# Strassen products for the gate and up projections, without GpSimd in the feed-forward; meta keys padded to 128 rows

## The chip, the cores and the metric

The kernel runs on one core of a Trainium2 chip. The metric is device microseconds of one execution; lower is better. The core's engines are TensorE (PE: matmuls; PEld: its weight loads), VectorE (DVE), ScalarE (ACT), GpSimd (POOL) and SyncE (SP, which issues the DMAs).

## The reference

A sequence of 512 tokens with 1024 features goes through a first block (two attention branches over the tokens and 16 "meta" tokens in front of them, 8 heads each) and then through two hybrid layers. Each hybrid layer has four mixing branches, an output projection and a gated feed-forward:

```python
x = x + merged.astype(dt) @ w_out
h2 = rms_norm(x, norm2_g)
ffn = (jax.nn.silu(h2 @ w_ffn_gate) * (h2 @ w_ffn_up)) @ w_ffn_down     # 1024 -> 2816 -> 1024
return x + ffn
```

## The kernel before

Activations lie transposed in SBUF: partitions are 128 features of a k-tile, the free axis is tokens. Every fp32 operand is split into a high part (a cast to fp32r) and a low part (the rest), and every product is three matmuls: high by high, high by low, low by high (`mm3`). Weights arrive by DMA into `raw` tiles (512 KB, three buffers); `split_w` casts 512 columns to `whi` on ACT and subtracts to get `wlo` on POOL (three buffers of each; with `k.lo` set, part or all of the subtractions go to DVE). `evict_split` does the same to a PSUM bank on ACT and DVE.

PE's order is the order of the program's text (a manual schedule). The order on the other engines is set at build time by a scheduler; each engine then runs its own queue in order, and waits on semaphores.

The feed-forward (`ffn`, line numbers from 1055 on) works on 22 blocks of 128 hidden features (`KF`). A block is a gate projection and an up projection, each 8 k-tiles by three matmuls of 512 tokens into one PSUM bank (`proj_t`, L248 to L250), then `silu2` (L353 ACT tanh, L354 DVE), a DVE multiply (L1067), a cast to `yh` (L1069 ACT) and a subtraction to `yl` (L1070 POOL). After every two blocks, `down` multiplies them by the down weights: two halves of 512 output features, four token tiles, three matmuls each (`proj_n`, L296 to L298), and `add_resid` (L497) adds each of the four banks to `x` on DVE. The whole of a `down` stands in PE's order between two projections. The last four blocks go through `proj_resid`, which also computes the sums of squares for the next norm; its weights are split by L557 (ACT) and L558 (POOL).

In front of the feed-forward, `proj_resid` for `w_out_2` ends each token tile with `norm_tile`: a norm (L527 DVE), eight transposes (L314 PE) and two `evict_split`s into `act`. The last tile's second half of this work runs inside the first gate block (`proj_late`, L278), which does tokens 0 to 255, the transposes, and then tokens 256 to 511 in 24 matmuls of 256 columns each.

In the first block, `Head.pv` (L443) multiplies probabilities by values for each of 16 heads, twice a head: keys in 128-row blocks, and first the 16 meta keys (`vm`, `pm`), with 16 rows on both operands.

Of the kernel before, what the change touches and what calls it, by code (L numbers as in the profile page):

```python
# [11 lines left out]
F32 = mybir.dt.float32  # L12
F32R = mybir.dt.float32r
AF = mybir.ActivationFunctionType
ALU = mybir.AluOpType
# [3 lines left out]
P = 128  # L19
S = 512  # L20
D = 1024
KD = D // P
# [45 lines left out]
class Task:  # L68
    def __init__(self, gen, cost):
        self.gen, self.left, self.done = gen, cost, False  # L70
# [89 lines left out]
def pe_cost(n):  # L160
    return max(n / 2.4 + 3, 110)
# [3 lines left out]
def hybrid_kernel(ctx: ExitStack, tc: tile.TileContext, i: dict, out: bass.AP):  # L165
# [59 lines left out]
    def raw_tile():  # L225
        return new(pool, [P, 1024], "raw", bufs=3)
# [8 lines left out]
    def w_cols(ap):  # L235

        loads, _, per, nk, _ = ap.shape
        for a in range(loads):
            raw = raw_tile().rearrange("p (m k c) -> p m k c", m=per, k=nk)
            nc.sync.dma_start(raw, ap[a])  # L240
            for m in range(per):
                yield raw[:, m]

    def mm3(ps, sh, sl, mh, ml, first, last):

        T_.matmul(ps, sh, mh, start=first, stop=False)  # L248
        T_.matmul(ps, sh, ml, start=False, stop=False)  # L249
        T_.matmul(ps, sl, mh, start=False, stop=last)  # L250

    def proj_t(outs, raw, nk):

# [142 lines left out]
    class Head:  # L396
# [7 lines left out]
        def trans(self, t, p, col):  # L404

            if t % 2 == 0:
                self.pt[t // 2] = [new(pool, [P, 4, 256], n, F32R) for n in ("pth", "ptl")]
                if self.meta:
                    k.pm_turn = 256 - k.pm_turn
                    self.pm[t // 2] = [a[0:NMETA, k.pm_turn:k.pm_turn + 256] for a in k.pm]  # L410
# [12 lines left out]
            if self.meta and t % 2:  # L423
                evict_split(self.pmt, *self.pm[t // 2])

        def pv(self, t):

# [95 lines left out]
    def norm_tile(x, t, ss, dst, gain):  # L523
# [12 lines left out]
        return second  # L536

    def proj_resid(get, ap, k0, nk, on_tile, delay=1):

        pss = [[bank(), bank()] for _ in range(NT)]  # L540
        for kk in range(nk - 4):
# [5 lines left out]
        ws = []  # L547
        for kk in range(nk - 4, nk):
            raw = load_w(ap, k0 + kk, 1, 0, D)[:, 0]
            if kk % 2:  # L550
# [84 lines left out]
def first_body(k, fb, col, hl):  # L635
# [63 lines left out]
        fox.rows = k.rows_out(fl, "frows")  # L699

    def v_tiles():
        v, vm = new(pool, [P, NT, 8, 2, 64], "v", F32R, 1), new(fb, [NMETA, 8, 2, 64], "vm", F32R)

        def put(t, ps, h0=0):
            src = ps.rearrange("p (h d) -> p h d", d=64)
            dst = (v[:, t] if t < NT else vm)[:, h0:h0 + src.shape[1]]
# [51 lines left out]
    def fox_values():  # L758
# [262 lines left out]
def hybrid_layer(k, spill, h, l, last):  # L1021
# [19 lines left out]
    def on_tile(t, pss):  # L1041
        for half, ps in enumerate(pss):
            k.add_resid(x, t, half, ps, ss)
        return k.norm_tile(x[:, t], t, ss, act, gain)

    k.proj_resid(lambda kk, t: tuple(a[:, kk, t * P:(t + 1) * P] for a in act), i["w_out_2"][l], 0, KD, on_tile)
    return ffn(k, x, l, act, last)


def ffn(k, x, l, h, last):  # L1050
    nc, i, new, V, A_, f, pool, bank, stream = k.nc, k.i, k.new, k.V, k.A_, k.f, k.pool, k.bank, k.stream
    gw, uw = (k.w_cols(i[n][l]) for n in ("t_gate", "t_up"))
    wd = i["w_ffn_down_2"][l]

    def get(kk):
        return h[0][:, kk], h[1][:, kk]

    def block(last=False):
        pg = bank()
        for _ in k.proj_t([(pg, get)], next(gw), KD):  # L1060
            pass
        gt = k.silu2(pg, k.t2())
        pu = bank()
        for _ in k.proj_t([(pu, get)], next(uw), KD):
            pass
        pr = k.t2()
        V.scalar_tensor_tensor(pr, pu, 0.5, gt, ALU.mult, ALU.mult)  # L1067
        hi, lo = k.y_tile()
        A_.copy(hi, pr)  # L1069
        (V if last else k.G).tensor_tensor(lo, pr, f(hi), ALU.subtract)  # L1070
        return hi, lo

    def down(a, acts):
        for half in range(2):
            pss = k.four()
            outs = [(pss[t], lambda kk, t=t: tuple(b[:, t * P:(t + 1) * P] for b in acts[kk])) for t in range(NT)]
            for _ in k.proj_n(outs, wd, len(acts), half * 512, 512, k0=a):
                pass
            for t in range(NT):
                k.add_resid(x, t, half, pss[t])  # L1080


    pending = None
    for a, n in [(a, 2) for a in range(0, KF - 4, 2)] + [(KF - 4, 4)]:
        acts = []
        for j in range(n):
            acts.append(block(j == 3))
            if pending:
                down(*pending)
                pending = None  # L1090
        pending = (a, acts)

    ss = new(k.small, [P, 8], "xss")
    gain = k.gain_row(i["final_g_2"] if last else i["norm1"][l + 1], "cb")
# [15 lines left out]
    k.proj_resid(lambda kk, t: tuple(b[:, t * P:(t + 1) * P] for b in acts[kk]), wd, KF - 4, 4, on_tile)  # L1110
    return (None, None) if last else (spill, h)


# [743 lines left out]
```

## Time and profile before

| | |
|---|---|
| time, median of three runs | 2608.05 us (2605.62 to 2610.39) |
| the profiled execution's own time, and its span | 2611.06 us; 2608.8 us |
[...]
| busy: PE, PEld, DVE, ACT, POOL | 2538.1, 2117.7, 1335.3, 1163.9, 1291.9 us |
| feed-forward of the first hybrid layer | about 1111 to 1486 us of the span |
| feed-forward of the second | about 2235 to 2609 us |

The span is from the first to the last instruction of the profiled execution; its time is a little longer, as it holds the launch around it. [...]

### The profile page before, as it was taken

Reading aid. Unit: us, or ns where it says so; the run is one execution under the profiler, and the core shown is the slowest. Engines: PE = TensorE matmul, PEld = TensorE weight load, DVE = VectorE, ACT = ScalarE, POOL = GpSimd, SP = SyncE. Lnnn points to the kernel's source line nnn. Section 1 sums busy time; section 2 is a strip of 40 time slices with the busy share of each in tenths; the row PEclk is TensorE's granted clock in tenths of the full one; section 3 lists DMA queues with packets and bytes.
Section 4 is the critical chain, followed back from the end, with each engine's and each line's share of the span. In section 5 each row is a group of like instructions: output and inputs, shape, how many; then the busy total and the mean of one; then the engine's idle time right before and its main releaser. Section 6 shows DMA issues by size and latency. Waiting matters only on the chain. (4 is left out here: it accounts for less than half of the span.)

```text
span 2608.8 us, 36327 instructions
## 1 busy us (share of the span) xinstructions
PE 2538.1 (97%) x12918; PEld 2117.7 (81%) x12918; DVE 1335.3 (51%) x2895; ACT 1163.9 (45%) x2533; POOL 1291.9 (50%) x1112
## 2 busy tenths in 40 slices
PE   7999999999999999999999999999999999999998
PEld 7878788888888878788888887888888877888887
DVE  4577547869436465522222469685355574322223
ACT  4567645447435444332222455365354453322223
POOL 3443245552466544455555555424665535455554
PEclk9999999999999999999999999999999999999999
DMA  5542242222437332322222332224364324222322
GB/s 152 147 127 65 75 134 95 80 88 64 137 105 188 112 109 82 137 89 97 97 96 93 110 108 76 88 64 121 118 187 119 99 88 143 82 92 96 97 97 89
DMA packets 117733, 276.98 MB, mean 106 GB/s; under 512 B 15824, under 2 KB 37584, under 8 KB 117552
## 3 DMA queue, kind: packets, MB, share of 16 engines
q1 hardware_dynamic: 117552, 274.65, 34.5%
q8 instruction: 103, 1.69, 0.3%
q14 instruction: 78, 0.64, 0.1%
HBM read 230.26 MB, written 6.46 MB: 91 GB/s over the span
## 5 line engine op out<-in xcount | busy, mean ns | idle before, releaser
L222 POOL TENSOR_TENSOR wlo<-raw,whi 128x512 fp32r<-128x512 f32 (+2 forms) x721 | 925.2, 1285 | 886.1 <-ACT whi L220 870.0
L220 ACT CAST whi<-raw 128x512 fp32r<-128x512 f32 (+2 forms) x733 | 445.0, 609 | 815.6 <-PE A L249 475.3
L248 PE MATMUL A<-hi,whi 128*128 128x512 f32 (+1 forms) x1848 | 741.0, 401 | 0.7 <-ACT hi L210 0.7
L250 PE MATMUL A<-hi,wlo 128*128 128x512 f32 (+1 forms) x1848 | 722.5, 391 | 6.0 <-POOL wlo L222 6.0
L249 PE MATMUL A<-lo,whi 128*128 128x512 f32 (+1 forms) x1848 | 724.4, 392 | 0.1
L250 PEld LDWEIGHTS A<-hi,wlo 128*128 128x128 f32 x1848 | 348.2, 188 | 85.6 <-POOL wlo L222 8.6
L248 PEld LDWEIGHTS A<-hi,whi 128*128 128x128 f32 x1848 | 348.5, 189 | 64.9 <-ACT hi L210 0.8
L249 PEld LDWEIGHTS A<-lo,whi 128*128 128x128 f32 x1848 | 348.6, 189 | 63.4 <-DVE lo L211 0.3
L314 PE MATMUL A<-ident,p 128*128 128x128 f32 (+3 forms) x1125 | 176.2, 279 | 31.3 <-DVE p L527 16.3
L497 DVE TENSOR_TENSOR x<-x,A 128x512 f32<-128x512 f32 x176 | 119.9, 688 | 157.7 <-PE A L298 96.4
L211 DVE TENSOR_TENSOR ptl<-A,pth 128x512 fp32r<-128x512 f32 (+3 forms) x256 | 149.1, 583 | 89.9 <-ACT pth L210 88.7
L314 PEld LDWEIGHTS A<-ident,p 128*128 128x128 f32 (+3 forms) x1125 | 135.2, 139 | 71.5 <-DVE p L527 17.7
L354 DVE SCALAR_TENSOR_TENSOR t<-t,A 128x512 f32<-128x512 f32 x44 | 30.3, 688 | 251.8 <-ACT t L353 251.8
L332 ACT ACTIVATE p<-p,sm 128x512 f32<-128x512 f32 (+6 forms) x160 | 100.6, 629 | 128.9 <-DVE sm L331 128.3
L210 ACT CAST pth<-A 128x512 fp32r<-128x512 f32 (+3 forms) x256 | 128.2, 501 | 64.9 <-PE A L314 64.2
L296 PE MATMUL A<-whi,hi 128*128 128x256 f32 (+7 forms) x440 | 144.2, 328 | 0.0
L310 POOL TENSOR_TENSOR rstd<-rstd,mhalf 128x1 f32<-128x1 f32 (+2 forms) x80 | 56.7, 710 | 175.5 <-DVE rstd L309 168.3
L298 PE MATMUL A<-whi,lo 128*128 128x256 f32 (+7 forms) x440 | 141.4, 321 | 0.0
L297 PE MATMUL A<-wlo,hi 128*128 128x256 f32 (+7 forms) x440 | 141.3, 321 | 0.0
L1067 DVE SCALAR_TENSOR_TENSOR t<-A,t 128x512 f32<-128x512 f32 x44 | 30.4, 692 | 172.5 <-PE A L250 172.5
L296 PE MATMUL A<-whi,yh 128*128 128x512 f32 x288 | 112.2, 390 | 0.0
L297 PE MATMUL A<-wlo,yh 128*128 128x512 f32 x288 | 112.2, 390 | 0.0
(365 smaller groups left out, 4565.5 us busy)
## 6 DMA issues: line engine op xcount, KB each, us to landing
raw<-in_t_gl_dram SPq DMA_DIRECT2D x64, 512.0 KB, 3.5
raw<-in_t_gate_dram SPq DMA_DIRECT2D x44, 512.0 KB, 3.4
raw<-in_t_up_dram SPq DMA_DIRECT2D x44, 512.0 KB, 3.5
raw<-in_w_ffn_down_dram SPq DMA_DIRECT2D x44, 512.0 KB, 3.7
raw<-in_w_in_dram SPq DMA_DIRECT2D x26, 512.0 KB, 3.7
raw<-in_w_out_dram SPq DMA_DIRECT2D x24, 512.0 KB, 3.6
ks<-sth SPq DMA_DIRECT2D x64, 128.0 KB, 2.4
ks<-stl SPq DMA_DIRECT2D x64, 128.0 KB, 2.3
```

The costliest lines, as they stand in the source:

```text
L210: A_.copy(hi, ps)
L211: V.tensor_tensor(lo, ps, f(hi), ALU.subtract)
L220: A_.copy(hi, src)
L222: (V if k.lo and k.turn % k.lo == 0 else G).tensor_tensor(lo, src, f(hi), ALU.subtract)
L248: T_.matmul(ps, sh, mh, start=first, stop=False)
L249: T_.matmul(ps, sh, ml, start=False, stop=False)
L250: T_.matmul(ps, sl, mh, start=False, stop=last)
L296: T_.matmul(ps, sh, wh[:, j], start=(b + j == 0), stop=False)
L297: T_.matmul(ps, sh, wl[:, j], start=False, stop=False)
L298: T_.matmul(ps, sl, wh[:, j], start=False, stop=(b + j == nk - 1))
L314: T_.transpose(dst, src, ident[0:k, 0:k])
L497: V.tensor_tensor(xx, xx, ps, ALU.add)
```

## The change

**Meta keys.** `vm` and `pm` get 128 partitions instead of 16, zeroed once by POOL memsets, so the meta matmuls contract over 128 rows.

**Quarters.** `norm_tile` in front of the feed-forward copies each transposed tile a second time, unsplit, to four fp32 "quarters" (k-tiles 0 to 3 or 4 to 7, tokens 0 to 255 or 256 to 511): eight ACT copies of 128x512 a layer.

**Gate and up by pairs of blocks.** Two blocks of a projection are a 2 by 2 product of quarters. `fast_pair` computes it in seven products instead of eight (Strassen's scheme in Winograd's form), each of 4 k-tiles by three matmuls of 256 tokens. `Tokens.sums` forms the four sums of token quarters once a layer and splits them; `fast_pair` forms four sums of weight quarters a pair (`s1` to `s4`) and splits the seven weight operands. Three PSUM banks (`px`, `pw`, `pz`) take the products, with ACT copies and DVE adds in between. The first pair's gate stays plain. So a layer has 21 fast pairs.

**Engines.** In the feed-forward every two-operand step stands on DVE (`k.lo` is 1; 2 during the plain pair), none on POOL until the last `proj_resid`.

**Down by fours.** `down` takes four blocks at a time and is a generator in the stream: after each product (12 matmuls) about one group of three 512-column matmuls is taken from it. It runs during the two pairs after its blocks are made; nothing runs between the products of the first two pairs.

```diff
     def v_tiles():
-        v, vm = new(pool, [P, NT, 8, 2, 64], "v", F32R, 1), new(fb, [NMETA, 8, 2, 64], "vm", F32R)
+        v, vm = new(pool, [P, NT, 8, 2, 64], "v", F32R, 1), new(fb, [P, 8, 2, 64], "vm", F32R)
+        G.memset(f(vm), 0.0)
...
     k.pm, k.pm_turn = k.y_tile(), 0
+    for a in k.pm:
+        G.memset(f(a), 0.0)
...
-                evict_split(ps.rearrange("p (j c) -> p j c", j=4), *(d[:, 4 * half:4 * half + 4, t * P:(t + 1) * P] for d in dst))
+                src = ps.rearrange("p (j c) -> p j c", j=4)
+                evict_split(src, *(d[:, 4 * half:4 * half + 4, t * P:(t + 1) * P] for d in dst))
+                if quarters:
+                    A_.copy(quarters[half][t // 2][:, :, (t % 2) * P:(t % 2 + 1) * P], src)
...
+        def sums(self):
+            (b11, b12), (b21, b22) = self.q
+            hi = new(pool, [P, 4, 4, 256], "v", F32R, 1)
+            lo = [new(pool, [P, 2, 4, 256], "ks", F32R) for _ in range(2)]
+            self.t = [(hi[:, j], lo[j // 2][:, j % 2]) for j in range(4)]
+            for c in (slice(0, 2), slice(2, 4)):
+                t = [t2().rearrange("p (k c) -> p k c", k=2) for _ in range(4)]
+                V.tensor_tensor(t[0], b12[:, c], b11[:, c], ALU.subtract)
+                V.tensor_tensor(t[1], b22[:, c], t[0], ALU.subtract)
+                V.tensor_tensor(t[2], b22[:, c], b12[:, c], ALU.subtract)
+                V.tensor_tensor(t[3], b21[:, c], t[1], ALU.subtract)
+                for j in (1, 2, 0, 3):
+                    A_.copy(self.t[j][0][:, c], t[j])
+                    V.tensor_tensor(self.t[j][1][:, c], t[j], f(self.t[j][0][:, c]), ALU.subtract)
...
+    def fast_pair(raw1, raw2, tok, dst):
+        a11, a21, a22, a12 = raw1[:, 0:4], raw2[:, 0:4], raw2[:, 4:8], raw1[:, 4:8]
...
+        A_.copy(h1, raw1)
+        V.tensor_tensor(l1, raw1, f(h1), ALU.subtract)
+        V.tensor_tensor(s1, a21, a22, ALU.add)
+        V.tensor_tensor(s2, s1, a11, ALU.subtract)
+        V.tensor_tensor(s3, a11, a21, ALU.subtract)
+        V.tensor_tensor(s4, a12, s2, ALU.subtract)
...
+        yield product(px, (h1[:, 0:4], l1[:, 0:4]), tok.quarter(0, 0))
+        A_.copy(q, px)
+        yield product(pw, (h1[:, 4:8], l1[:, 4:8]), tok.quarter(1, 0))
+        V.tensor_tensor(d1[:, 0:256], q, pw, ALU.add)
+        yield product(px, split(s2), t2_, False)
+        A_.copy(u2, px)
+        yield product(pz, split(s1), t1)
+        A_.copy(z, pz)
+        yield product(px, split(s3), t3, False)
+        V.tensor_tensor(d2[:, 256:512], z, px, ALU.add)
+        yield product(pz, split(s4), tok.quarter(1, 1), False)
+        V.tensor_tensor(d1[:, 256:512], u2, pz, ALU.add)
+        yield product(px, split(a22), t4, False)
+        A_.copy(d2[:, 0:256], px)
...
+    def fast(w):
+        dst = [k.t2() for _ in range(2)]
+        for cost in k.fast_pair(next(w), next(w), tok, dst):
+            stream.run(cost * rate)
+        return dst
...
+        if first:
+            k.lo = 2
+            gts = [k.silu2(plain(gw), k.t2()) for _ in range(2)]
+            tok.sums()
+            k.lo = 1
+        else:
+            gts = [k.silu2(g, g) for g in fast(gw)]
...
+    rate = 2 * NT * 2 * 3 * k.pe_cost(S) / (14 * 12 * k.pe_cost(256))
```

Two places show what moves on DVE. The first is the start of the feed-forward in the first hybrid layer. Before, DVE's queue from the first gate block on holds (`t` is the silu's and the product's tile, `A` a PSUM bank, `x` the residual):

```order
L354 SCALAR_TENSOR_TENSOR t_2664_12233<-t_2665_12234,A_12160 128x512
L1067 SCALAR_TENSOR_TENSOR t_2672_12272<-A_12237,t_2664_12233 128x512
L354 SCALAR_TENSOR_TENSOR t_2681_12313<-t_2682_12314,A_12278 128x512
L1067 SCALAR_TENSOR_TENSOR t_2689_12352<-A_12317,t_2681_12313 128x512
L354 SCALAR_TENSOR_TENSOR t_2698_12393<-t_2699_12394,A_12358 128x512
L1067 SCALAR_TENSOR_TENSOR t_2706_12432<-A_12397,t_2698_12393 128x512
```

Now, behind the second gate block's silu, the queue goes on with the token sums (L560 to L563, `t`; first their columns c = 0 to 1, then 2 to 3) and their low parts (L566, `ks`); ahead of these rows stand the silu and three sums `t_2681`, `t_2682`, `t_2683`. The third product of the first fast pair needs the low parts of the second sum, made from `t_2682` and `t_2686`:

```order
L566 TENSOR_TENSOR ks_12293<-t_2681_12295,v_12292 128x512
L563 TENSOR_TENSOR t_2684_12298<-cst_11794,t_2682_12296 128x512
L587 TENSOR_TENSOR ptl_12622<-raw_12613,pth_12621 128x1024
L560 TENSOR_TENSOR t_2685_12311<-qs_11793,qs_11792 128x512
L566 TENSOR_TENSOR ks_12293<-t_2682_12296,v_12292 128x512
L566 TENSOR_TENSOR ks_12294<-t_2683_12297,v_12292 128x512
L566 TENSOR_TENSOR ks_12294<-t_2684_12298,v_12292 128x512
L561 TENSOR_TENSOR t_2686_12312<-cst_11795,t_2685_12311 128x512
L566 TENSOR_TENSOR ks_12293<-t_2685_12311,v_12292 128x512
L562 TENSOR_TENSOR t_2687_12313<-cst_11795,qs_11793 128x512
L563 TENSOR_TENSOR t_2688_12314<-cst_11794,t_2686_12312 128x512
L588 TENSOR_TENSOR p_12477<-qs_12475 128x512
```

The next row is `ks_12293<-t_2686_12312`. What moved: where the queue held one or two instructions a block, each behind a matmul, it now holds a run of 16 between the second gate's silu and that row.

The second place is the middle of the feed-forward. Before, DVE's queue there is two multiplies a block and the adds to `x`:

```order
L354 SCALAR_TENSOR_TENSOR t_2750_12637<-t_2751_12638,A_12602 128x512
L1067 SCALAR_TENSOR_TENSOR t_2758_12676<-A_12641,t_2750_12637 128x512
L497 TENSOR_TENSOR x_11778<-x_11778,A_12682 128x512
L497 TENSOR_TENSOR x_11778<-x_11778,A_12683 128x512
L497 TENSOR_TENSOR x_11778<-x_11778,A_12684 128x512
```

Now (`wlo` from L581 is the low part of a product's weights, from L222 that of the down weights; L588 to L591 are the sums for the next pair; L606 and L612 add a product's bank):

```order
L606 TENSOR_TENSOR t_2880_13293<-t_2893_13314,A_13312 128x256
L222 TENSOR_TENSOR wlo_13394<-raw_13328,whi_13393 128x512
L581 TENSOR_TENSOR wlo_13402<-p_13301,whi_13401 128x512
L590 TENSOR_TENSOR p_13483<-raw_13477,qs_13479 128x512
L581 TENSOR_TENSOR wlo_13422<-p_13302,whi_13421 128x512
L498 TENSOR_TENSOR x_11782<-x_11782,A_13150 128x512
L591 TENSOR_TENSOR p_13484<-raw_13477,p_13482 128x512
L612 TENSOR_TENSOR t_2881_13294<-t_2894_13315,A_13311 128x256
L581 TENSOR_TENSOR wlo_13442<-qs_13297,whi_13441 128x512
```

What moved: the subtractions that POOL did, and all new sums, stand in one DVE queue, 40 instructions for a gate pair and an up pair together, and each `wlo` is awaited by the product after it.

## Rows read from the trace of the kernel before

**Rows 1.** Windows of both feed-forwards: stretch, us, busy us (instructions), PEclk, DMA, GB/s
```profile
1118.00:1456.00 338.00, 338.00 (x1472) 275.86 (x1471) 78.77 (x115) 103.50 (x172) 190.93 (x149) 1.00 0.30 99
2241.00:2580.00 339.00, 339.00 (x1479) 276.75 (x1478) 79.08 (x116) 103.51 (x172) 191.37 (x150) 1.00 0.30 97
```

**Rows 2.** Groups of 1118 to 1456: busy us, mean ns | idle before, releaser
```profile
L222 POOL TENSOR_TENSOR wlo<-raw,whi 128x512 fp32r<-128x512 f32 x121 | 156.4, 1293 | 150.2 <-ACT whi L220 150.2
...
L220 ACT CAST whi<-raw 128x512 fp32r<-128x512 f32 x121 | 75.2, 621 | 223.5 <-PE A L249 149.2 <-PE A L298 68.7 <-PE A L250 2.4
...
L497 DVE TENSOR_TENSOR x<-x,A 128x512 f32<-128x512 f32 x72 | 49.1, 688 | 48.0 <-PE A L298 48.0
...
L558 POOL TENSOR_TENSOR ptl<-raw,pth 128x512 fp32r<-128x512 f32 x4 | 5.1, 1302 | 1.4 <-ACT pth L557 1.4
```

**Rows 3.** PE alone, a stretch of down, then of gate and up
```profile
1150.00:1157.25 7.25, 7.25 (x33) 1.00 0.21 72
1157.25:1179.52 22.27, 22.27 (x98) 1.00 0.28 95
```

**Rows 4.** Timeline of PE, second pass of the first gate block
```profile
1115.63 0.39 PE L278 MATMUL A<-hi,whi 128*128 128x256 f32 x1
1115.86 0.28 PE L278 MATMUL A<-hi,wlo 128*128 128x256 f32 x1
...
1117.62 1.11 PE L278 MATMUL A<-lo,whi 128*128 128x256 f32 x8
1118.56 0.40 PE L248 MATMUL A<-hi,whi 128*128 128x512 f32 x1
```

**Rows 5.** Timeline of PE around one meta multiplication in the first block
```profile
85.11 0.39 PE L250 MATMUL A<-hi,wlo 128*128 128x512 f32 x1
85.43 0.38 PE L443 MATMUL A<-yh,vm 16*128 16x256 f32 x1
85.65 0.27 PE L443 MATMUL A<-yl,vm 16*64 16x256 f32 x1
85.85 0.39 PE L443 MATMUL A<-pth,v 128*128 128x256 f32 x1
86.08 0.34 PE L443 MATMUL A<-ptl,v 128*64 128x256 f32 x2
```

**Rows 6.** Timeline of DVE, two independent instructions in a row
```profile
690.10 1.28 DVE L211 TENSOR_TENSOR v<-A,v 128x512 fp32r<-128x512 f32 x2
```

**Rows 7.** Instructions of line 222: count, ns min/median/max, first and last start
```profile
L222 DVE TENSOR_TENSOR wlo<-raw,whi x12: 680/690/1469, 551.7 to 1704.7; 128x512 fp32r<-128x512 f32 x12
```

**Rows 8.** Groups on DVE over the whole span, by shape
```profile
L211 DVE TENSOR_TENSOR ptl<-A,pth 128x256 fp32r<-128x256 f32 x48 | 19.9, 414 | 30.2 <-ACT pth L210 30.2
...
L1152 DVE TENSOR_TENSOR x<-x,t 128x512 f32<-128x512 f32 x16 | 25.4, 1587 | 0.2
```

**Rows 9.** Timeline of ACT and DVE at the end of the first gate block
```profile
1118.35 0.62 ACT L220 CAST whi<-raw 128x512 fp32r<-128x512 f32 x1 [2.04 <-PE A L278]
...
1118.87 0.59 ACT L353 ACTIVATE t<-A 128x512 f32<-128x512 f32 x1
...
1119.50 0.69 DVE L354 SCALAR_TENSOR_TENSOR t<-t,A 128x512 f32<-128x512 f32 x1 [2.46 <-ACT t L353]
```

**Rows 10.** Busy time and granted clock after two long waits of PE
```profile
358.00:365.00 7.00, 5.75 (x28) 5.74 (x29) 5.51 (x13) 2.49 (x6) 1.38 (x3) 0.52 0.31 120
...
412.70:416.10 3.40, 3.35 (x8) 2.67 (x9) 1.56 (x7) 2.13 (x6) 2.48 (x2) 0.52 0.46 154
```

**Rows 11.** Timeline of PE at those two waits
```profile
359.25 1.11 PE L314 MATMUL A<-ident,p 128*128 128x128 f32 x4 [4.07 <-DVE p L527]
...
412.75 0.80 PE L250 MATMUL A<-hi,wlo 128*128 128x512 f32 x1 [2.16 <-POOL wlo L222]
```

**Rows 12.** Groups on POOL over the whole span
```profile
L1282 POOL MEMSET p<- 36x512 f32 x2 | 1.0, 518 | 0.0
```

**Rows 13.** Timeline of PE at the start of the span
```profile
7.28 1.12 PE L314 MATMUL A<-ident,p 128*128 128x128 f32 x4 [7.28 <-DVE p L527]
```

More of the change, by code (lines that the diff above doesn't have):

```diff
@@ L233, in load_w, with w_cols @@
         return raw
-    def w_cols(ap):
+    def w_cols(ap, other=None):
         loads, _, per, nk, _ = ap.shape
         for a in range(loads):
-            raw = raw_tile().rearrange("p (m k c) -> p m k c", m=per, k=nk)
+            raw = (other() if other and a > 2 and a % 2 else raw_tile()).rearrange("p (m k c) -> p m k c", m=per, k=nk)
             nc.sync.dma_start(raw, ap[a])
@@ L242, in w_cols, with mm3 @@
                 yield raw[:, m]
[L246 to L250, printed above, removed]
+    def mm3(ps, sh, sl, mh, ml, first, last, **kw):
+        T_.matmul(ps, sh, mh, start=first, stop=False, **kw)
+        T_.matmul(ps, sh, ml, start=False, stop=False, **kw)
+        T_.matmul(ps, sl, mh, start=False, stop=last, **kw)
     def proj_t(outs, raw, nk):
@@ new lines, in fast_pair, with part, split, product @@
+    def fast_pair(raw1, raw2, tok, dst):
+        a11, a21, a22, a12 = raw1[:, 0:4], raw2[:, 0:4], raw2[:, 4:8], raw1[:, 4:8]
+        def part():
+            return p_tile().rearrange("p (k c) -> p k c", k=4)
+        def split(src):
+            hi, lo = (new(pool, [P, 512], t, F32R, 3).rearrange("p (k c) -> p k c", k=4) for t in ("whi", "wlo"))
+            A_.copy(hi, src)
+            V.tensor_tensor(lo, src, f(hi), ALU.subtract)
+            return hi, lo
+        s1, s2, s3, s4 = (part() for _ in range(4))
+        h1, l1 = (new(pool, [P, 4, 256], n, F32R).rearrange("p a b -> p (a b)").rearrange("p (k c) -> p k c", k=KD) for n in ("pth", "ptl"))
+        A_.copy(h1, raw1)
[4 more added lines that the diff above has]
+        V.tensor_tensor(s4, a12, s2, ALU.subtract)
+        t1, t2_, t3, t4 = tok.t
+        px, pw, pz = (bank()[:, 0:256] for _ in range(3))
+        def product(ps, w, m, first=True):
+            for j in range(4):
+                mm3(ps, w[0][:, j], w[1][:, j], m[0][:, j], m[1][:, j], first and j == 0, j == 3, skip_group_check=not first)
+            return 12 * pe_cost(256)
+        (u, v), (d1, d2) = (t2(), t2()), dst
+        q, u2, z = u[:, 0:256], u[:, 256:512], v[:, 0:256]
+        yield product(px, (h1[:, 0:4], l1[:, 0:4]), tok.quarter(0, 0))
[12 more added lines that the diff above has]
+        A_.copy(d2[:, 0:256], px)
@@ L1050, in ffn, with plain, y_tiles, pair @@
-def ffn(k, x, l, h, last):
+    return ffn(k, x, l, act, quarters, last)
+def ffn(k, x, l, h, quarters, last):
     nc, i, new, V, A_, f, pool, bank, stream = k.nc, k.i, k.new, k.V, k.A_, k.f, k.pool, k.bank, k.stream
-    gw, uw = (k.w_cols(i[n][l]) for n in ("t_gate", "t_up"))
+    gw, uw = (k.w_cols(i[n][l], lambda: new(pool, [P, 2 * L], "qs")[:, 0:1024]) for n in ("t_gate", "t_up"))
+    tok = k.Tokens(h, quarters)
     wd = i["w_ffn_down_2"][l]
+    count = [0]
     def get(kk):
         return h[0][:, kk], h[1][:, kk]
-    def block(last=False):
-        pg = bank()
-        for _ in k.proj_t([(pg, get)], next(gw), KD):
-            pass
[L1062 to L1071, printed above, removed]
+    def plain(w):
+        ps = bank()
+        for _ in k.proj_t([(ps, get)], next(w), KD):
+            pass
+        return ps
+    def fast(w):
[3 more added lines that the diff above has]
+        return dst
+    def y_tiles():
+        count[0] += 1
+        if count[0] % 8 == 0:
+            return [new(pool, [P, L], n, F32R, 1)[:, 0:S] for n in ("sth", "stl")]
+        if count[0] % 8 == 4:
+            return [k.gate_tile().bitcast(F32R) for _ in range(2)]
+        return k.y_tile()
+    def pair(first):
+        if first:
[5 more added lines that the diff above has]
+            gts = [k.silu2(g, g) for g in fast(gw)]
+        out = []
+        for u, gt in zip(fast(uw), gts):
+            V.scalar_tensor_tensor(gt, u, 0.5, gt, ALU.mult, ALU.mult)
+            hi, lo = y_tiles()
+            A_.copy(hi, gt)
+            V.tensor_tensor(lo, gt, f(hi), ALU.subtract)
+            out.append((hi, lo))
+        return out
@@ L1076, in down @@
             outs = [(pss[t], lambda kk, t=t: tuple(b[:, t * P:(t + 1) * P] for b in acts[kk])) for t in range(NT)]
-            for _ in k.proj_n(outs, wd, len(acts), half * 512, 512, k0=a):
-                pass
+            yield from k.proj_n(outs, wd, len(acts), half * 512, 512, k0=a)
             for t in range(NT):
                 k.add_resid(x, t, half, pss[t])
[L1083 to L1091, printed above, removed]
+    rate = 2 * NT * 2 * 3 * k.pe_cost(S) / (14 * 12 * k.pe_cost(256))
+    acts = []
+    for a in range(0, KF, 2):
+        acts += pair(a == 0)
+        if len(acts) >= 4 and a < KF - 4:
+            stream.drain()
+            stream.push(down(a + 2 - len(acts), acts), 0)
+            acts = []
+        elif a == KF - 4:
+            stream.drain()
+            stream.push(down(KF - 6, acts[0:2]), 0)
+            acts = acts[2:]
+    stream.drain()
+    k.lo = 0
     ss = new(k.small, [P, 8], "xss")
@@ L1108, in on_tile, with home @@
             nc.sync.dma_start(k.out[t * P:(t + 1) * P, sl], x[:, t, sl])
-    k.proj_resid(lambda kk, t: tuple(b[:, t * P:(t + 1) * P] for b in acts[kk]), wd, KF - 4, 4, on_tile)
+    homes = iter(((pool, "qs"), (k.mix, "cst")))
+    def home():
+        where, tag = next(homes)
+        return tuple(new(where, [P, 1024], tag, F32R, 2) for _ in range(2))
+    k.proj_resid(lambda kk, t: tuple(b[:, t * P:(t + 1) * P] for b in acts[kk]), wd, KF - 4, 4, on_tile, home=home)
     return (None, None) if last else (spill, h)
```

24 lines of the change are left out of this document (16 added, 8 removed).

## The prediction, made before the change had run

> **What bounds the kernel now.** I began with the windows by stage, because the share of busy time over a whole span hides its stages. In both feed-forwards PE is busy for all of the stretch, 338.00 of 338.00 us and 339.00 of 339.00, at the full granted clock, while DVE has 79 us of work, ACT 104 and POOL 191, and the DMA engines are busy for 0.30 [rows 1]. The groups say who waits for whom: POOL's subtractions (L222) stood idle 150.2 us for the casts (L220), and most idle time of these was a wait for PE's banks [rows 2]. So PE is the bound, and what counts is how long it needs from one matmul's start to the next. PE alone gives that: 96 gate and up matmuls of 512 columns in 22.27 us, 0.232 us a step, and 32 of down in 7.25, 0.227 [rows 3]. The two extra records of the first and the one extra of the second are neighbours cut by the window.
>
> **1. The products: -51 us.** Two plain blocks are 48 matmuls of 512 columns, 48 x 0.232 = 11.13 us. A fast pair is 7 x 12 = 84 matmuls of 256 columns. The trace has such matmuls in this very role: the second pass of the first gate block runs 8 of them, with new weights each, from 1117.62 to the next start at 1118.56, (1118.56 - 1117.62) / 8 = 0.118 us; the whole pass of 24 takes 1118.56 - 1115.63 = 2.93 us, 0.122 [rows 4]. At 0.118 the pair is 9.91 us, 1.22 less; 42 pairs (21 a layer) give -51. At 0.122 they would give -37, at half of 0.232, the lowest I can think of, -58. The weight loads grow from 48 to 84 a pair, and PEld has one for each matmul already [rows 1].
>
> [...] The steps of 0.118 in rows 4, each with weights of its own on all 128 rows, leave no room for a load in line, so I give it no chance.
>
> **2. The meta keys: -10 us.** In `pv` the step into the first meta matmul is 85.43 - 85.11 = 0.32 where a full matmul of 512 has 0.232, and the steps around it are 0.22, 0.20 and 0.23 where 256 columns of 128 rows take 0.118 [rows 5]. That is (0.32 - 0.232) + (0.22 + 0.20 + 0.23 - 3 x 0.118) = 0.39 us a call; with 32 calls (16 heads, twice) 12.4 us. Some calls will stand where PE waits for something else, so I take 10; bounds 0 and 12.4. [...] The zeroing is 4 memsets, about 2 us of POOL by the nearest row (518 ns for 36x512, [rows 12]), in the first microseconds, while PE's first work waits 7.28 us for a norm anyway [rows 13].
>
> **3. The start of a feed-forward: +13 us a layer, +26.** This is where a new wait arises. The second gate block's silu ends about 1.6 to 2.3 us after PE leaves that block: 1119.50 + 0.69 - 1118.56 = 1.63 at the first block [rows 9], and 0.6 more if a cast of 0.62 stands ahead. Behind it DVE has 16 rows until the low part of the second token sum: 15 of 512 columns and one of 1024. For one I have 0.69 [rows 2, 7] and, back to back, 1.28 - 0.68 = 0.60 [rows 6]; for 1024 columns at most twice that. [...] By rows the 16 take 15 x 0.60 + 1.2 = 10.2 to 15 x 0.69 + 1.38 = 11.7 us, so the sum stands at 11.8 to 14.0. PE meanwhile has two products and half of the third, 30 matmuls, 3.5 us. It waits 8.3 to 10.5 us; I take 9.7. To this come 0.7 at the seventh product, whose bank is read by L612 behind more DVE rows; 1.0 in the second pair, which has no down beside it, so DVE has 24 x 0.66 + 6 x 0.42 + 2 x 1.2 = 20.8 us of work (0.42: [rows 8]) against 168 x 0.118 = 19.8 of PE; and 1.3 for the clock: after a wait of 4.07 us PE ran at 0.52 for about 7 us, and after one of 2.16 us for 3.4 [rows 10, 11]. That is 12.7, say 13; bounds 9 and 18. Behind the waiting matmul stand all later products, and the silu, casts and down that need them, so nothing makes it up.
>
> **4. The steady state: +4 us.** From the third pair on, a gate and an up pair with their down take PE 168 x 0.118 + 48 x 0.227 = 30.7 us. DVE has 40 instructions for it: 32 of 512 columns, 6 of 256 and 2 of 1024, by the same rows 26 us at 0.66 (27 at 0.69); ACT has 28, at 0.62 about 17. POOL's 1293 ns subtractions [rows 2] are gone. So DVE would be 85% busy, in one queue, with PE waiting for each `wlo`. `whi` and `wlo` have three buffers, and the tight places are those where a buffer comes free with one product and is needed for the low part of one soon after: 12 x 0.118 of a product, 3 x 0.227 of down and two matmuls ahead of the reader, 2.3 us from release to need. Against that stand a release of 0.31 (1118.87 - 1118.56, [rows 9]), a cast of 0.62, a subtraction of 0.69, 0.04 between them as between tanh and silu there, and 0.2 that I add for the hand-over to PE: 1.9 us, with DVE free at that moment. Where DVE is in the middle of another 0.69, it is late by 0.3. I take 0.1 a fast pair for the 36 with a down: +3.6; bounds 0 and 22 (0.3 at two places of a pair).
>
> **5. The end: +2 us.** The last `proj_resid` splits its weights with POOL subtractions of 1302 ns (L558, [rows 2]) as before, but beside DVE work on two SBUF operands, which can take 1587 ns where POOL is busy (L1152, [rows 8]). I take 1 us a layer, 0 to 3. The eight quarter copies a layer are ACT work of 0.6 us at a place where ACT is busy 0.31 of the time [rows 1]; if the transposes' banks came free later by one of them, 0.6 a layer, inside these bounds. Weights come by the same DMA count, and the engines were at 0.30.
>
> **The sum.** -51.2 - 10 + 26 + 3.6 + 2 = -29.6. The profiled execution took 2611.06 us, so 2581.5 on its scale; the median of the runs is 3.0 below it, 2578.5. Forecast 2579.
>
> **The rivals.**
> A, the start's wait is hidden, since DVE gets through its 16 rows while the second gate block still runs. For it: the early sums need only tokens that are ready. Against: the silu stands ahead of them in the queue, and waits for PE. It saves about 23: 2556. Chance 0.08.
> B, the forecast. Own range 2566 to 2594. Chance 0.55.
> C, the other side: DVE becomes the bound of the steady state. Its work there is 26 / 0.66 = 39.4 times a 512-column instruction, so it passes PE's 30.7 us at a mean of 0.78 us, and eats the whole gain (29.6 over 20 gate-and-up rounds, 1.5 us each) at 0.82. For it: L1152 shows 1.59 us for two SBUF operands beside POOL, and L222's longest is 1.47 [rows 7, 8]. Against: POOL is almost idle there now, and the median is 0.69. At 0.85 a round is 33.5, +2.8 over 20 rounds: 2635. Chance 0.12.
> D, the change doesn't do what it says: half-wide matmuls don't come at half price in short runs, because each product's first step, into another bank, costs a full 0.23. For it: the first steps of the pass, 0.23 and on average 0.122 [rows 4]. Against: the 8 behind. 0.11 x 7 x 42 = +32: 2611. Chance 0.13.
> E, the tight places of the steady state bind at each pair, +0.3 at two of them, +22 instead of +3.6: 2597 to 2604. Chance 0.12.
>
> **How the numbers follow.** Some 0.2% (2602.8 to 2613.3) is what a measurement of this kernel can tell from no change. A, B and E are faster: 0.75. D is nearly all in the band: 0.10 of its 0.13 same, the rest slower, with C: 0.15. The terms' bounds taken together reach from 2555 to 2635; without C and the upper side of D, 2552 to 2612 keeps 0.8.
>
> **What would show it.** In the profile after: the steps inside products near 0.118 and PE's feed-forward busy time down by a tenth (1); steps of 0.118 in `pv` with no 0.2 (2); in each feed-forward one or two waits of PE, 9 to 10 us together, in the first products of the first fast pair, released by DVE's L566 (or L587), with a half clock behind (3); DVE 80 to 90% busy in the middle, its 512-column instructions at 0.60 to 0.69, and PE's waits there under 0.2 us each (4). The prediction is wrong if those DVE instructions exceed 0.78, if PE's waits in the middle come at every pair, or if the first step of each product is 0.2.

## The result, and the profile after

The changed kernel takes 2580.7 us, median of four runs (2576.7 to 2581.96); the kernel before took 2609.2 (2605.6 to 2611.6). The ratio is 0.9891, 95% interval 0.9877 to 0.9906. The forecast was 2579, with the sign right; the terms behind it came out less well than their sum.

To see where the time went, both traces were cut at five matmuls that exist in both: the first 512-column matmul behind each `proj_late` (in the first hybrid layer, its feed-forward's second gate block, and the same in the second layer) and the last matmul.

| stretch, us | before | after | change |
|---|---|---|---|
| start (with all meta keys) to the first layer's first projection | 369.75 | 358.21 | -11.54 |
| to the second gate block of the first feed-forward | 748.81 | 754.04 | +5.23 |
| this feed-forward, to the second layer's first projection | 370.98 | 357.24 | -13.74 |
| to the second gate block of the second feed-forward | 752.60 | 754.55 | +1.95 |
| to the last matmul | 359.29 | 347.37 | -11.92 |

So the first block gave 11.5 us and the feed-forwards 25.7, and 7.2 went in the two mixing stretches, which the change touches only at their ends (quarter copies, and the first pair's weight sums). The windows of both feed-forwards, from the second fast pair to near the end, answer to [rows 1] (columns as there):

```profile
1150.00:1430.00 280.00, 280.00 (x1973) 262.14 (x1973) 223.39 (x362) 138.89 (x260) 5.56 (x4) 1.00 0.31 101
2260.00:2540.00 280.00, 279.30 (x1969) 261.44 (x1968) 223.69 (x362) 138.90 (x261) 4.23 (x4) 1.00 0.32 103
```

PE is still the bound, with no idle time in the first and 0.7 us in the second. DVE went from 23% of such a stretch to 80%, ACT from 31% to 50%, POOL from 56% to 2%. The groups of DVE between 1150 and 1430 us (busy us, mean ns | idle before, releaser) answer to [rows 2, 7]:

```profile
L581 DVE TENSOR_TENSOR wlo<-p,whi 128x512 fp32r<-128x512 f32 x73 | 50.2, 687 | 3.3 <-ACT whi L580 1.1
L222 DVE TENSOR_TENSOR wlo<-raw,whi 128x512 fp32r<-128x512 f32 x36 | 25.2, 699 | 33.2 <-ACT whi L220 33.0
L498 DVE TENSOR_TENSOR x<-x,A 128x512 f32<-128x512 f32 x37 | 25.2, 680 | 0.0
L587 DVE TENSOR_TENSOR ptl<-raw,pth 128x1024 fp32r<-128x1024 f32 x17 | 20.8, 1223 | 5.4 <-ACT pth L586 5.2
```

The mean of a 512-column row is 0.69 us, far from the 0.78 at which DVE would have become the bound, and the 1024-column row takes 1.22, not twice 0.69.

The start of the first feed-forward is where PE waits. Its timeline from the end of the second product on:

```profile
1120.53 0.28 PE L251 MATMUL A<-hi,ptl 128*128 128x256 f32 x1
1128.12 0.58 PE L249 MATMUL A<-v,whi 128*128 128x256 f32 x1 [7.31 <-ACT t L604]
1128.49 0.41 PE L250 MATMUL A<-ks,whi 128*128 128x256 f32 x1
...
1129.56 0.41 PE L249 MATMUL A<-v,whi 128*128 128x256 f32 x1
1130.12 0.58 PE L250 MATMUL A<-ks,whi 128*128 128x256 f32 x1
...
1133.06 0.34 PE L251 MATMUL A<-v,wlo 128*128 128x256 f32 x1
1133.24 0.28 PE L249 MATMUL A<-v,whi 128*128 128x256 f32 x1
...
1136.42 0.28 PE L249 MATMUL A<-v,whi 128*128 128x256 f32 x1
...
1137.84 0.28 PE L249 MATMUL A<-hi,pth 128*128 128x256 f32 x1
```

Three things stand in these rows. PE is idle for 7.3 us in front of the third product, and ACT's copy L604 releases it. Its eighth matmul, the first that reads the low part of the second sum's later half (`ks`), comes 0.56 us after the seventh instead of 0.21: the wait that the prediction had put there, now a remainder of 0.35. And from 1128.12 to 1133.06 the steps are 0.213 (0.37 and 0.38 behind the two stops) where the later ones are 0.118: behind the wait the granted clock is 0.50 in 1128.1 to 1133.0, and 0.99 in 1133.1 to 1136.4. The third and fourth products should have started at 1120.65 and taken 24 x 0.118 = 2.83 us; the fifth starts at 1133.60, so the start costs 1133.60 - 1120.65 - 2.83 = 10.1 us: 7.5 of wait, 0.35, and about 2.3 of half clock. The seventh product (1136.42 to 1137.84, 12 steps of 0.118) and the pair behind it run without a wait.

DVE and ACT at the same place:

```profile
1119.10 0.68 DVE L355 SCALAR_TENSOR_TENSOR t<-t,A 128x512 f32<-128x512 f32 x1
1119.69 0.68 DVE L560 TENSOR_TENSOR t<-qs,qs 128x512 f32<-128x512 f32 x1
...
1124.57 1.89 DVE L566 TENSOR_TENSOR ks<-t,v 128x512 fp32r<-128x512 f32 x3
1126.37 0.68 DVE L561 TENSOR_TENSOR t<-cst,t 128x512 f32<-128x512 f32 x1
1126.97 0.68 DVE L566 TENSOR_TENSOR ks<-t,v 128x512 fp32r<-128x512 f32 x1
...
1128.78 0.68 DVE L588 TENSOR_TENSOR p<-qs 128x512 f32<-128x512 f32 x1
1129.38 1.28 DVE L566 TENSOR_TENSOR ks<-t,v 128x512 fp32r<-128x512 f32 x2
```

```profile
1127.09 0.62 ACT L565 CAST v<-t 128x512 fp32r<-128x512 f32 x1 [1.79 <-DVE t L561]
1127.69 0.37 ACT L604 COPY t<-A 128x256 f32<-128x256 f32 x1
```

DVE runs its rows back to back, a row every 0.60 us. Counted along the queue shown with the change, the low part of the second sum's later half (from `t_2686`) is the row right behind L588, the first of the two at 1129.38. It ends at 1130.06, and the eighth matmul of the third product, which reads it, starts at 1130.12. The copy that frees the bank `px` for the third product needs only the first product, done at 1119.4, but stands on ACT behind the cast L565 of the same half of that sum (L561), which DVE gets to at 1126.37.

So the copy decides where PE stops, at the product's first matmul, and DVE's 16 rows decide when the eighth can go. At 0.118 a step the eighth, 31 matmuls behind 1117.81, would have started at 1121.47; it is 8.65 us late. The other 1.5 of the 10.1 us are half clock behind it. By this count a copy in time would have brought seven matmuls forward and left the eighth where it is.

The meta multiplication of [rows 5], after:

```profile
84.75 0.39 PE L251 MATMUL A<-hi,wlo 128*128 128x512 f32 x1
84.99 0.28 PE L444 MATMUL A<-yh,vm 128*128 128x256 f32 x1
85.10 0.28 PE L444 MATMUL A<-yl,vm 128*64 128x256 f32 x1
85.22 0.28 PE L444 MATMUL A<-pth,v 128*128 128x256 f32 x1
85.33 0.33 PE L444 MATMUL A<-ptl,v 128*64 128x256 f32 x2
```

The steps are 0.24, 0.11, 0.12 and 0.11, where they were 0.32, 0.22, 0.20 and 0.23.

### The profile page after: what moved, and what is told of

It is laid out like the page before. It is cut to its first block, busy times and chain, and to the rows that moved or that the text cites. A ratio compares the mean times of both kernels' runs of the same rounds, so it can differ in the third digit from the quotient of the medians.

```text
span 2578.9 us, 39966 instructions
## 1 busy us (share of the span) xinstructions
PE 2489.7 (97%) x14430; PEld 2158.1 (84%) x14430; DVE 1718.3 (67%) x3527; ACT 1294.7 (50%) x2817; POOL 934.0 (36%) x830
## 4 chain that ended last, share of the span: by engine, by line
PE 63%; DVE 11%; DMA 3%; issue 2%; ACT 2%; POOL 2%; SPq 0%; DVEq 0%; POOLq 0%; ACTq 0%
PE A L249 14%; PE A L250 14%; PE A L251 14%; PE A L297 4%; PE A L299 4%; PE A L298 4%; PE A L315 3%; PE A L444 2%; DMA raw<-in_w_out_dram 1%; DVE x L1277 1%; PE A L489 1%; DVE ptl L211 1%; POOL wlo L222 1%; DVE sm L332 1%; POOL ptl L640 1%
## 5 line engine op out<-in xcount | busy, mean ns | idle before, releaser
L222 POOL TENSOR_TENSOR wlo<-raw,whi 128x512 fp32r<-128x512 f32 (+4 forms) x477 | 612.8, 1288 | 583.0 <-ACT whi L220 567.3
L220 ACT CAST whi<-raw 128x512 fp32r<-128x512 f32 (+4 forms) x565 | 340.8, 605 | 507.7 <-PE A L250 320.1
L249 PE MATMUL A<-hi,whi 128*128 128x512 f32 (+2 forms) x1344 | 524.6, 390 | 0.7 <-ACT hi L210 0.7
L251 PE MATMUL A<-hi,wlo 128*128 128x512 f32 (+2 forms) x1344 | 505.6, 376 | 3.1 <-POOL wlo L222 2.9
L250 PE MATMUL A<-lo,whi 128*128 128x512 f32 (+2 forms) x1344 | 505.9, 376 | 0.1
L251 PEld LDWEIGHTS A<-hi,wlo 128*128 128x128 f32 x1344 | 253.6, 189 | 54.6 <-POOL wlo L222 6.1
L249 PE MATMUL A<-v,whi 128*128 128x256 f32 x672 | 191.9, 286 | 15.3 <-ACT t L604 14.6
L251 PE MATMUL A<-v,wlo 128*128 128x256 f32 x672 | 191.1, 284 | 0.2 <-DVE wlo L581 0.2
L250 PE MATMUL A<-ks,whi 128*128 128x256 f32 x672 | 191.0, 284 | 0.3
L222 DVE TENSOR_TENSOR wlo<-raw,whi 128x512 fp32r<-128x512 f32 x88 | 64.5, 733 | 125.8 <-ACT whi L220 125.6
L249 PEld LDWEIGHTS A<-v,whi 128*128 128x128 f32 x672 | 129.1, 192 | 21.9 <-ACT t L604 15.0
```

The source lines that it names most:

```text
L220: A_.copy(hi, src)
L222: (V if k.lo and k.turn % k.lo == 0 else G).tensor_tensor(lo, src, f(hi), ALU.subtract)
L249: T_.matmul(ps, sh, mh, start=first, stop=False, **kw)
L250: T_.matmul(ps, sh, ml, start=False, stop=False, **kw)
L251: T_.matmul(ps, sl, mh, start=False, stop=last, **kw)
```

## The experiments

The theory under test: the padding gives about 10 us and the products 51; the start of each feed-forward gives 20 of that back, through DVE's queue; the steady state costs next to nothing. The rivals: other parts of the change make the gain; or the start's cost is DVE's whole work and not the order of its rows; or DVE is at its limit all along. Ratios are against the kernel before, with 95% intervals.

### The padding alone, and the change without it

```diff
+        v, vm = ..., new(fb, [P, 8, 2, 64], "vm", F32R); G.memset(f(vm), 0.0)   # e1: into the kernel before
-        v, vm = ..., new(fb, [P, 8, 2, 64], "vm", F32R); G.memset(f(vm), 0.0)   # e2: out of the changed one
```

(Shortened; the same is done with `pm`.)

> The kernel before with only the meta keys padded to 128 rows. Theory: the shorter first block of the changed kernel (about 11 us between the same two matmuls of the two traces) is the padding's alone, so about 2598 us (2595 to 2601), with steps of 0.118 us around the meta matmuls. Rival: the first block got shorter through other timing, and the padding only moves PE's time into waits for other engines; then the time stays within 4 us of 2609.

> The changed kernel with the meta keys at 16 rows again. Theory: the padding's 11 us come back and nothing else, 2592 us (2589 to 2595), and the feed-forwards keep their length within 1 us. Rival: the padding is worth less beside the rest, below 2586.

The padding alone: 2598.9 us, ratio 0.9962 (0.9948 to 0.9977), 10.3 us less than before. The change without it: 2590.4, ratio 0.9923 (0.9907 to 0.994), 9.7 more than with it. The two parts of the change add up, and the padding is worth 10 us. Both times lie in the theories' ranges.

### All blocks plain, the rest of the change kept

```diff
     def fast(w):
-        dst = [k.t2() for _ in range(2)]
-        for cost in k.fast_pair(next(w), next(w), tok, dst):
-            stream.run(cost * rate)
-        return dst
+        for _ in range(2):
+            ps = bank()
+            for cost in k.proj_t([(ps, get)], next(w), KD):
+                stream.run(cost * 0.5)
+            yield ps
...
-            tok.sums()
```

> The changed kernel with all gate and up blocks as plain products and without the token sums; the quarter copies, the engines' division and the down by fours between the products stay. Theory: the products alone give 42 x 1.22 = 51 us, and the start costs about 10 us a layer, so without both the time is 2581 + 51 - 20 = 2612 us (2607 to 2616), and no wait of PE over 1 us is left in the feed-forward. Rival: part of the gain comes from the division of engines and the down by fours, then at most 2603 us.

2632.9 us, ratio 1.0091 (1.0074 to 1.0108): 21 more than the theory's figure, and on the other side from the rival. The row of PE's waits in the first feed-forward says why (us, times, longest):

```profile
PE A L298 <- DVE wlo L222: 8.9, 18, 1.1
```

Beside plain blocks the split of the down weights comes 0.61 us late at nearly every half of a down, and the step behind it is 0.1 longer: all steps over 0.32 us of this feed-forward together, less 0.23 each, come to 14.4 us. That fault is this experiment's own: the changed kernel has no such wait. Without it the first feed-forward is 386.6 - 14.4 = 372.2 us against 371.0 before (1.8 of it in such steps), so by this subtraction the division of engines and the down by fours gain nothing by themselves. And against 357.24 - 10.1 = 347.1 of the changed kernel (without its start) the products gain 25 a layer, where 21 x 1.22 = 25.6 were predicted. No run has plain blocks without the fault; that the steps of the products are 0.118 is read from the changed kernel's trace itself.

### The start, in five forms

First only the place of the work changes: the first pair's up blocks plain (e4); the sums between the two plain gate blocks (e5); both (e6).

```diff
-        for u, gt in zip(fast(uw), gts):
+        for u, gt in zip((plain(uw) for _ in range(2)) if first else fast(uw), gts):      # e4, e6
...
-            gts = [k.silu2(plain(gw), k.t2()) for _ in range(2)]
+            gts = [k.silu2(plain(gw), k.t2())]                                            # e5, e6
             tok.sums()
+            gts += [k.silu2(plain(gw), k.t2())]
```

> The changed kernel with the first pair's up blocks plain too; the token sums are formed beside them, and the first fast pair is the second gate pair. Theory: the start's wait is DVE's run of rows while PE has only 3.5 us of work, and 11 us more of matmuls cover it; per layer 10.3 us of wait and half clock go and 1.2 us of a lost fast pair come, 18 us for both: 2562 us (2557 to 2567). Rival: the rows of the sums and of the next pairs' weights form one queue that is late wherever the first fast pair stands; the wait moves there, and the time is 2578 to 2584 us.

> The changed kernel with the token sums written between the two plain gate blocks instead of behind them; all instructions are the same. Theory: the wait of 7.5 us at the third product is DVE's run of 16 rows, which starts only behind the second gate block's silu; now it starts behind the first one's, 5.6 us sooner, so that the wait falls to about 2 us and the half clock behind it mostly goes: 10.3 us a layer become about 3, in all 2567 us (2562 to 2572). Rival: what counts is DVE's whole work up to the third product, not where the sums stand in it; then other rows (the weights' sums) are late instead, and the time is 2575 to 2581 us.

> The run before with the first pair's up blocks plain, and the token sums between the two plain gate blocks. Theory: PE has 17 us of plain matmuls beside DVE's sums, and no wait over 1 us is left at the first fast pair; 10.3 us a layer go and 1.2 come for the lost fast pair: 2562 us (2557 to 2567). Rival: DVE's total work at the start is the limit (in the run with the first up blocks plain it had no idle time for 25 us and the wait was still 5.8 us); then 2572 to 2579 us.

e4: 2578.4 us, ratio 0.9885 (0.987 to 0.9899). The rival's figure: the wait moved to the first fast pair, 5.8 us, behind the cast of the weights' second sum, which DVE formed only at 1137.35; it had run without idle time since 1119.8.

e5: 2578.2, ratio 0.9879 (0.9864 to 0.9894). Again the rival's: the sums start 5.6 us sooner against the second gate block (1114.77 - 1112.89 = 1.9 us behind its start instead of 1119.69 - 1112.25 = 7.4), and the wait is 7.0 instead of 7.3. In ACT's timeline the same copy has another row ahead:

```profile
1127.39 0.62 ACT L565 CAST v<-t 128x512 fp32r<-128x512 f32 x1 [1.72 <-DVE t L563]
1128.00 0.37 ACT L604 COPY t<-A 128x256 f32<-128x256 f32 x1
```

It is now the cast of the fourth sum (L563), which no product needs before the seventh. DVE's timeline shows the same on the other engine:

```profile
1122.53 0.68 DVE L561 TENSOR_TENSOR t<-cst,t 128x512 f32<-128x512 f32 x1
1123.13 1.29 DVE L566 TENSOR_TENSOR ks<-t,v 128x512 fp32r<-128x512 f32 x2
1124.33 0.69 DVE L562 TENSOR_TENSOR t<-cst,qs 128x512 f32<-128x512 f32 x1
1124.94 1.22 DVE L587 TENSOR_TENSOR ptl<-raw,pth 128x1024 fp32r<-128x1024 f32 x1
1126.07 0.68 DVE L588 TENSOR_TENSOR p<-qs 128x512 f32<-128x512 f32 x1
1126.67 0.68 DVE L563 TENSOR_TENSOR t<-cst,t 128x512 f32<-128x512 f32 x1
1127.28 0.68 DVE L566 TENSOR_TENSOR ks<-t,v 128x512 fp32r<-128x512 f32 x1
```

In this kernel's queue the two rows at 1123.13 are low parts of the fourth and the first sum. The low part that the third product needs is the row at 1127.28, done at 1127.96: it stands behind six rows (4.1 us) that this product doesn't need, among them a low part (L587) of a later pair's weights. The copy on ACT ends at 1128.37, and the eighth matmul starts at 1130.08. So a copy in time would have brought that matmul forward by 2.1 us at most; the rest is DVE, and there the order of its rows.

e6: 2566.2, ratio 0.984 (0.9824 to 0.9856), near the theory's 2562. The waits of PE in the first feed-forward:

```profile
PE A L251 <- DVE wlo L581: 2.1, 2, 1.8
PE A L251 <- DVE yl L1185: 1.0, 1, 1.0
PE A L249 <- DVE t L612: 0.2, 1, 0.2
```

1.8 us are left at the first fast pair, with some 17 steps at half clock (0.213 us) behind them.

Then the order itself, on top of e5 (e9) and of e6 (e10): the sums stand in place in the quarters, those of the third and fourth products are split first in the text, the others behind the second product. The text sets PE's order alone; DVE's and ACT's queues are the scheduler's.

```diff
-                for j in (1, 2, 0, 3):
-                    A_.copy(self.t[j][0][:, c], t[j])
-                    V.tensor_tensor(self.t[j][1][:, c], t[j], f(self.t[j][0][:, c]), ALU.subtract)
+            raw = [[q[:, c] for c in cs] for q in (b11, b22, b12, b21)]    # the sums replace the quarters
...
+                split(1, n)
+            for n in range(2):
+                split(0, n)
+            def later():      # called behind the second product
+                for n, c in enumerate(cs):
+                    split(2, n)
+                for n, c in enumerate(cs):
+                    V.tensor_tensor(raw[3][n], b21[:, c], raw[1][n], ALU.subtract)
+                    split(3, n)
```

> The run with the sums between the two plain gate blocks, with the sums that the third and fourth products need formed and split first, in place in the quarters, and the splits of the other two written behind the second product; as many instructions as before. Theory: in the earlier run the wait stayed 7.0 us because the copy that frees the first product's bank stood on ACT behind the cast of the fourth sum, which no product needs until the seventh; without that row ahead the wait at the third product falls under 3 us, and the time to 2566 to 2573 us. Rival: DVE's whole work is the limit, as it was busy without a break from the first gate's silu to the fourth product; the wait only moves to a later product, 2575 to 2581 us.

> The same order of the sums, and the first pair's up blocks plain. Theory: the last wait of 1.8 us at the first fast pair goes with the rows ahead of it, and the half clock behind it (some 2 us) too, 4 us a layer: 2559 us (2555 to 2564). Rival: that wait was for the weights' sums, which still stand behind as many rows; then as the run without the new order, 2564 to 2568 us.

e9: 2574.5, ratio 0.987 (0.9853 to 0.9886), between the two figures. PE's waits fall from 7.0 to 4.0 in both feed-forwards, and the feed-forward stretches are 2.3 and 3.4 us shorter than e5's; the intervals of the two times overlap. The copy is in time now. The waits that are left, in the first feed-forward, and DVE's rows there:

```profile
1122.12 0.39 PE L250 MATMUL A<-ks,whi 128*128 128x256 f32 x1 [1.39 <-DVE ks L563]
...
1125.73 0.58 PE L250 MATMUL A<-ks,whi 128*128 128x256 f32 x1 [2.63 <-DVE ks L563]
```

```profile
1119.65 0.68 DVE L577 TENSOR_TENSOR cst<-cst,cst 128x512 f32<-128x512 f32 x1
1120.25 1.21 DVE L601 TENSOR_TENSOR ptl<-raw,pth 128x1024 fp32r<-128x1024 f32 x1
1121.39 0.68 DVE L563 TENSOR_TENSOR ks<-cst,v 128x512 fp32r<-128x512 f32 x1
1121.99 1.28 DVE L563 TENSOR_TENSOR ks<-qs,v 128x512 fp32r<-128x512 f32 x2
1123.19 0.68 DVE L577 TENSOR_TENSOR cst<-cst,cst 128x512 f32<-128x512 f32 x1
1123.79 0.68 DVE L595 TENSOR_TENSOR wlo<-p,whi 128x512 fp32r<-128x512 f32 x1
1124.40 0.68 DVE L355 SCALAR_TENSOR_TENSOR t<-t,A 128x512 f32<-128x512 f32 x1
```

Both waits are in the third product still, at its second and eighth matmul, for the two low parts of the second sum: the row at 1121.39, and the one right behind those shown. The scheduler has put rows ahead of them that the third product doesn't need: a fourth sum (L577) and a later pair's low part (L601), 1.7 us; then third and fourth sums, the fifth product's weights and the silu, 3.0 us. So the order of the rows, on DVE and ACT together, is worth the 3 us of wait that e9 takes, and what is left is order too by the same count. That DVE's whole work is the limit, as the rival had it, is not shown: DVE is busy without a break from 1108.9 to 1132.3, but no run has a queue in which only needed rows stand ahead, nor one that changes the order on one engine alone. e10: 2567.7, ratio 0.984 (0.9826 to 0.9855), the rival's figure and not the theory's. No wait over 1 us is left, and its feed-forward stretches are 3.1 and 1.9 us shorter than e6's (349.7 and 339.0 against 352.8 and 340.9); but its mixing stretches are 4.2 and 3.7 longer, and the medians are the same. e6 and e10 are faster than the changed kernel, their intervals against the kernel before lie apart from its, and no order of them is shown.

### Less work for DVE, and a down in one piece

```diff
-            k.lo = 1
+            k.lo = 0                       # e7
...
-            stream.run(cost * rate)
+            stream.run(1e9)                # e8
```

> The changed kernel with the down weights' low parts on POOL again (4 of the 40 DVE instructions of a gate and an up pair). Theory: PE is the bound and DVE has slack, so taking 2.4 us from DVE's 24 gains nothing (2579 to 2582 us), and POOL beside DVE only makes both slower. Rival: DVE's two-operand instructions run at 1.5 us instead of 0.68 beside POOL; 5 us of POOL in each 31 would make PE wait at these places, 2585 to 2600 us.

> The changed kernel with the whole down (96 matmuls) behind the first product of the next pair instead of spread between the products. Theory: the first pairs, which have no down beside them, ran in the changed kernel without a wait of PE, so DVE keeps up with products alone, and the spread is worth little: 2579 to 2586 us. Rival: DVE has about 19 us of work for 19.8 us of products, any late row stops PE, and 9 stretches of three bare pairs a layer cost 2 to 4 us each: 2600 to 2640 us.

e7: 2579.35, ratio 0.9886 (0.9872 to 0.9901), no different from the changed kernel. The groups between 1150 and 1430 us show the contention, and that it is covered:

```profile
L581 DVE TENSOR_TENSOR wlo<-p,whi 128x512 fp32r<-128x512 f32 x73 | 58.1, 796 | 46.6 <-ACT whi L580 46.6
...
L222 POOL TENSOR_TENSOR wlo<-raw,whi 128x512 fp32r<-128x512 f32 x36 | 54.1, 1503 | 249.2 <-ACT whi L220 192.7 <-PE A L299 56.5
```

796 ns is the mean of all 73 rows (687 in the changed kernel): the 19 that overlap a POOL subtraction take 0.96 to 1.44 us, 1.12 on average, the others at most 0.70. POOL's take 1503, and PE has no idle time in this stretch. Both parts of the theory hold. e8: 2583.4, ratio 0.9903 (0.9887 to 0.992), 2.7 us above the changed kernel, with overlapping intervals. DVE is busy for the same 80% of a stretch with bare pairs of products in it, and among these pairs PE has one wait of 1.1 us near the end of each feed-forward. So the steady state has slack, and the spread of the down is worth little.

### The mixing stretches, once more

Both kernels were profiled again, unchanged (2612.8 and 2582.4 us in one run each).

> The kernel before, unchanged, once more, for one stage: from the first feed-forward-like stage to the second gate block of the first hybrid layer it took 748.8 us in the first trace, and 749.5 to 755.8 in ten traces of kernels whose queues hold the same rows there. Theory: the length of this stage differs from execution to execution, at the place where PE waits for a copy by DMA and a softmax; then it lies anywhere in 748 to 756. Rival: it belongs to the kernel, as the start of the feed-forward's work on DVE and other addresses come in; then 748 to 750 again.

> The changed kernel, unchanged, once more, for the same stage (754.0 us in the first trace). Theory: it differs from execution to execution, anywhere in 748 to 756. Rival: it belongs to the kernel, 753 to 756 again, about 1 us of it at the end of the stage, where DVE already forms sums for the first fast pair.

The kernel before: 749.4 and 752.0 us for the two stretches (748.8 and 752.6 at first); the changed one: 753.1 and 756.9 (754.0 and 754.6). These are the rival's figures, and e1, which leaves the feed-forward as before (750.4 and 752.6), fits them: the longer stretches go with the changed kernel. But the theory's range holds all of them too, and the others with the new feed-forward have 749.5 to 755.8 and 752.4 to 758.2, so the kernel alone doesn't settle the length. Matched matmul by matmul, about 1 us of the first stretch is lost in the last tiles of `proj_resid` in front of the feed-forward and 0.6 between the last tile's transposes and the second gate block, where DVE already forms the first pair's weight sums. Some 3 us are lost at one place in each layer, in the middle of a mixing branch. PE's waits there, in the changed kernel:

```profile
PE A L1759 <- DVE sm L334: 1.8, 1, 1.8
PE A L1760 <- DMA ks<-stl: 0.4, 1, 0.4
```

The trace before has only the second of them (0.4 us). In the first layer every engine's queue holds the same rows in the same order up to there, apart from the memsets and two neighbours early on DVE. What is late first is DVE's subtraction into `stl`, released by a copy DMA's end 5.2 us after its issue, where it had been 4.3. Why this copy takes longer, and why the loss is in most traces of the new kernels but not in e3's and e6's, stays open.

## Why the prediction was right, point by point

1. **The products, -51: right.** The steps are 0.118 in all products, the first of each too, and 25 us a layer are gained (e3, by subtraction). D is out. So is a load in line: between 1150 and 1430 us PEld has 1973 loads for PE's 1973 matmuls, 188 to 190 ns each, and the products step at 0.118 all the same.
2. **The meta keys, -10: right**, 10.3 alone and 9.7 within the change (e1, e2). (The prediction's sum gives 0.38 a call and not 0.39, 12.3 in all.)
3. **The start, +26: right in place and cause, too dear.** It cost 10.1 us a layer instead of 13. The wait for DVE's rows was sized well: the silu ended 1.97 us behind its block (1.6 to 2.3 were said), the 16 rows took 10.4 us (10.2 to 11.7), and the matmul that needs the last of them came 8.65 us late (8.3 to 10.5 were said, 9.7 taken). The half clock behind that matmul cost 1.5 (1.3 taken). What was too dear is 1.0 in the wait, and the 0.7 at the seventh product and the 1.0 in the second pair, which didn't come. What the prediction didn't see is the copy on ACT, queued behind a cast: PE stopped at the third product's first matmul and not in its middle, so the first seven matmuls ran late and at half clock too, inside the same 8.65 us. A is out by the wait.
4. **The steady state, +4: right in size, partly by luck.** Its waits come to 0.4 us in the first feed-forward and about 1.3 in the second, where 3.6 were taken. Beside them the down matmuls, in groups between products, start every 0.230 us instead of 0.227 ([rows 3]; in one piece, in e8, 0.227 again), 1.3 us a layer that the sum lacked. C and E are out. (The casts of [rows 2] write SBUF, so what they waited for on PE was a `whi` buffer that its matmuls still read, and not a bank; nothing in the sums hangs on it. The 0.2 for the hand-over to PE was an estimate without a row; behind the low part that ended at 1130.06 PE's eighth matmul started 0.06 later.)
5. **The end, +2: right within its bounds**: 0.6 us a layer at the late tile (it lies in the mixing stretch), and no new wait behind the last pair over 0.5 us.

The total was close partly because two errors met: the start was 6 us too dear, and the mixing stretches, costed at nothing but for the late tile, took 7. Why they did is open in the main.

## What to carry to other kernels

When work moves to an engine with slack, its mean share says little: DVE at 80% stopped PE only at the one place where many rows fell due at once, and the half clock behind the wait cost about 2.3 us more. There, lay more work of the bound engine beside the burst (e6), and look in every queue of the chain for rows that nobody needs yet: in e5 and e9 the scheduler had put some ahead of the awaited ones on DVE, and in e5 on ACT too, and taking part of them away took 3 us off the wait. The engine named as the releaser need not be the one that sets the time: here a copy on ACT released PE, and DVE held it at the eighth matmul all the same. Padding a short contraction to the full 128 rows can be worth more than its zeros cost: 10 us over 32 calls.

## What the runs showed of the hardware that was not expected

A DVE row on two SBUF operands that overlaps a POOL subtraction takes 1.12 us on average instead of 0.68, and POOL's row 1503 ns instead of 1293 [rows 2] (e7). DVE's mean of 796 ns hides that: one row of four takes the whole of it. Behind a wait of 1.8 us (e6) the granted clock was 0.52 in the 3.5 us from 1129.0 on (steps of 0.213), behind one of 1.4 us (e9) it was 1.00 in 1122.2 to 1123.1 (steps of 0.12). And 512-column matmuls in groups of three between 256-column products start 3 ns later each than in one piece (0.230 and 0.227 us).
